# A decoder step on one core: the TensorE order of its attention fixed by the program, with other PSUM shares and another pace of the work beside it

## The chip, the cores and the metric

The kernel runs on one core of one Trainium2 chip. The metric is the device time of one execution in microseconds (us), as the median of several runs. One further execution was recorded instruction by instruction; it is called the profiled execution.

## The reference, cut to what matters

One inference step of a decoder with two layers, for two groups of tokens: a new sequence of 2048 tokens (the prompt), and 8 running sequences with 8 new tokens each (the sample), whose 4096 older positions lie in a paged cache. The first layer is recurrent. The second is attention with a forget term, for 16 heads of 64 columns; the prompt attends to itself, the sample to its cache and itself.

```python
def fox_block(q, k, v, cq, ck, q_pos, k_pos):
    s = jnp.einsum('bqhd,bkhd->bhqk', q, k).astype(jnp.float32) * (HEAD_DIM ** -0.5)
    s = s + jnp.swapaxes(cq, 1, 2)[:, :, :, None] - jnp.swapaxes(ck, 1, 2)[:, :, None, :]
    mask = k_pos[None, :] <= q_pos[:, None]
    s = jnp.where(mask[None, None], s, -jnp.inf)
    p = jax.nn.softmax(s, axis=-1)
    return jnp.einsum('bhqk,bkhd->bqhd', p.astype(v.dtype), v)
...
    return (o * jax.nn.silu(g)) @ w_out
```

All data are float32.

## The kernel before, in words

The program runs in stages: the recurrent layer, the projections to keys, values, queries and gates (with the sample's attention started beside the last of them), the prompt's attention, and the output projection. This case is about the prompt's attention, `attention` (from L1304), and the sample's, `decode` (from L1013), which runs beside it.

**The prompt's attention.** The loop at L1523 runs over 64 units (16 heads, 4 blocks of 512 query columns each), and within a unit over the key blocks k of 128 rows that the causal mask leaves: 640 steps in all, one step being one block of scores.
- *Scores* `st` (L1531, L1532, and L1534 for the mask on the diagonal): two matmuls of up to 512 columns into one PSUM bank. ScalarE takes the exponential into a tile `p` or `acc` (L1540).
- *Maxima* `sx` (`top`, L1404): before a unit's scores can be made, each of its query rows needs a maximum. One matmul of up to 512 columns into a PSUM bank is reduced by VectorE (L1406, or with the mask L1408). There are 640 of these too. `tops` gathers a unit's maxima (L1417), transposes them on TensorE (`mps`, L1421) and ScalarE writes them as rows of the queries `qbt` (L1423). `advance` issues the maxima some steps ahead of the unit that needs them, two for each step while there are any to do.
- *Products* `ops` (L1551): four steps' exponentials times the values, sixteen recorded matmuls. They are issued two steps after the fourth exponential. GpSimd adds the exponentials up (L104, `acc`), and the sums are turned into a divisor by `total` and `norm` (`tot` L1454, `rp` L1478).

**The sample's attention.** `decode` does 16 turns, 14 of them here. A turn reads 8 groups of four cache pages of keys and 8 of values, 1 MB each, into one of four buffers `raw` (DMA at L1072). VectorE transposes the keys into `ktr` (L1157); the score matmuls `dS` (L1125) and, for the new tokens, L1140 follow, then a softmax, a trip of the weights through DRAM (`pd`, `sx`), and the products `dO` (L1235), collected by `dres` (L1263). `Side.along` steps this generator forward in proportion to the cost that the loop at L1523 yields; `share` at L1796 is the proportion.

**What sets the order.** The program is written in one order, but it is built with a scheduler that runs the whole program in its own simulated time and puts on each engine, as the next instruction, one that it holds to be ready there; program order is only the priority. The result is a fixed queue for each engine. `together` (L106) keeps the matmuls of one group behind the group's first; nothing else holds TensorE's instructions in the program's order. On the chip each engine takes its queue from the front, and the DMAs are in SyncE's queue.

**PSUM.** Eight banks. The pool of the attention has six: one for `ops`, two for the scores `st`, three under the name `sx` for the maxima, `mps`, `tot` and `rp` in turn. The sample has the other two, `d` and `o`.

Of the kernel before, what the change touches and what calls it, by code (L numbers as in the profile page):

```python
# [11 lines left out]
F32 = mybir.dt.float32  # L12
# [8 lines left out]
P = 128  # L21
# [6 lines left out]
H = 16  # L28
# [16 lines left out]

SHARE = 1.13
LEAD = 18
RAMP = 8
# [4 lines left out]
FIRST = 2  # L53
NACC = 5
NP = 5
ADD = "G"
# [17 lines left out]

SYNC = mybir.DependencyInfo(mybir.DependencyClass.Sync, mybir.DependencyReason.DATA)


# [6 lines left out]
def tile_hawk_fox(  # L84
# [18 lines left out]
    def tt(eng, out, a, b, op):  # L103
        eng.tensor_tensor(out, a, b, op=op)  # L104

    def together(mms, after=()):  # L106

        first = mms[0]().ins
        for d in after:
            tc.add_manual_dep(first, d.ins.name, SYNC)  # L110
        with tc.high_priority(), tc.issue_after(first):
            for mm in mms[1:]:
                mm()

# [96 lines left out]
    psum = {}  # L211
# [1095 lines left out]
    def attention(es):  # L1307
# [3 lines left out]
        ops2 = ps3.tile([P, 512], F32, name="ops", tag="ops", bufs=1)  # L1311
        ps3.tile([P, 512], F32, name="st", tag="st", bufs=2)
        pool.tile([P, 512], F32, name="acc", tag="acc", bufs=NACC)
# [80 lines left out]
        def top(u, j, ck):  # L1394
# [7 lines left out]
            w = 512 if ck < qc else (j + 1) * P  # L1402
            ps = ps3.tile([P, 512], F32, name="sx", tag="sx", bufs=3)
            T.matmul(ps[:, :w], qb[0:96, j * P:(j + 1) * P], kb[0:96, ck * 512:ck * 512 + w], start=True, stop=True)  # L1404
            if ck < qc:
# [7 lines left out]
        def tops(u):  # L1413

            h, qc = units[u]
            m = mrows[u % 2]
            V.tensor_reduce(m[:, :4], mxs.pop(u)[:, :, :qc + 1], axis=AX.X, op=ALU.max)  # L1417

            def row():
                ps = ps3.tile([P, 512], F32, name="mps", tag="sx", bufs=3)  # L1420
                T.transpose(ps[:, :P], m[:, :], ident[:, :])  # L1421
                for j in range(4):
                    A.mul(qbs[u % NQ][96:100, j * P:(j + 1) * P], ps[:4, :P], less[:, j:j + 1])  # L1423

            later.after(1, row)
# [23 lines left out]
        def total(h2, sums, todo, single):  # L1449


            ps = ps3.tile([P, 512], F32, name="tot", tag="sx", bufs=3)
            for qc, acc in todo:
# [11 lines left out]
        def norm(pr, sums, q0, n, oT):  # L1465
# [10 lines left out]
            def gate(qc, sg):  # L1476
                ps = ps3.tile([P, 512], F32, name="rp", tag="sx", bufs=3)
# [43 lines left out]
        ops = acc = None  # L1521
        pair = []
        for u, (h, qc) in enumerate(units):  # L1523
            load_low(u + 2)
            for k in range(nks[u]):
# [3 lines left out]
                ks = slice(k * P, (k + 1) * P)  # L1529
                ps = ps3.tile([P, 512], F32, name="st", tag="st", bufs=2)  # L1530
                T.matmul(ps[:, lo:], ka[:, ks], qa[:, lo:], start=True, stop=False)  # L1531
                T.matmul(ps[:, lo:], kb[:, ks], qb[:, lo:], start=False, stop=(k < qc * 4))  # L1532
# [42 lines left out]

    lent = {}

# [18 lines left out]
    def project(es):  # L1596
# [22 lines left out]
        def post(i, pool, yps, x1, y):  # L1619
# [9 lines left out]
            if i < len(rows) - 1:  # L1629
# [9 lines left out]
                     y=lent["out"][:, :, :].rearrange("p k d -> p (k d)"),  # L1639
                     ps=lambda j: lent["psum"].tile([P, 512], F32, name="y", tag="st", bufs=2))]  # L1640

# [153 lines left out]
    psum["att"] = banks(att, "psa", 6)  # L1795
    side.along(attention(att), share)  # L1796
    side.upto(1e12)
# [38 lines left out]
```

## Time and profile before

| | us |
|---|---|
| three runs | 3064.86, 3054.63, 3062.46 |
| their median | 3062.46 |
| the profiled execution | 3055.27 |
| its span, from the first to the last instruction | 3053.6 |
| TensorE (PE) busy in the span | 2827.0 (93%) |
| VectorE (DVE) busy | 1810.2 (59%) |
| ScalarE (ACT) busy | 1269.8 (42%) |
| GpSimd (POOL) busy | 1079.6 (35%) |
| the prompt's attention, about | 1715 to 2850 in the span |
| the sample's last product in it | 2559.9 |

In the lines of the profile, L1404 is line 1404 of the kernel before; `out<-in` are the program's names of tiles. Busy time of PE is modelled from the matmul's size, and matmuls overlap, so two of them in a row show 0.39 us each while they start 0.23 us apart. "PEclk" is the share of the full TensorE clock that was granted. A wait is an idle time of an engine and what ended it.

### The profile page before, as it was taken

What the parts mean: (1) busy time and instruction counts of PE and PEld (TensorE: products, weight loads), DVE (VectorE), ACT (ScalarE), POOL (GpSimd) and SP (SyncE); (2) the same over time, 40 slices, a digit from 0 to 9 for tenths busy, and PEclk for the clock granted to TensorE, in tenths of its full rate; (3) what the DMA queues carried; (4) which work ended last, traced back from release to release, by engine and by line L of the source; (5) the groups of instructions that cost most, each with busy time, mean ns of one, the idle gap of its engine ahead of it and who ended that gap; (6) DMA issues with size and microseconds to landing.
All of it is one profiled execution on the core that took longest, in us unless ns stands there. A gap on an engine that the chain in (4) does not pass through costs nothing.

```text
span 3053.6 us, 60463 instructions
## 1 busy us (share of the span) xinstructions
PE 2827.0 (93%) x21614; PEld 2258.5 (74%) x21614; DVE 1810.2 (59%) x4012; ACT 1269.8 (42%) x2874; POOL 1079.6 (35%) x1199
## 2 busy tenths in 40 slices
PE   6998999999999989998999799899899899999898
PEld 5997789988999978896888456565556565565687
DVE  7876465425357766765555566676767675554344
ACT  4665442222346655433333144343444345455311
POOL 1653201000016532000000366556465557587522
PEclk9999999999999999999999799899999999999999
DMA  4224546788622256999999988999999998323243
GB/s 122 81 85 133 175 125 203 240 268 263 216 83 89 83 185 194 316 320 320 330 311 315 294 274 268 299 275 308 306 298 319 322 297 258 92 65 86 84 145 111
DMA packets 492864, 653.41 MB, mean 214 GB/s; under 512 B 91099, under 2 KB 292828, under 8 KB 485285
## 3 DMA queue, kind: packets, MB, share of 16 engines
q1 hardware_dynamic: 488934, 643.87, 67.1%
q10 hardware_dynamic: 3340, 3.56, 0.5%
q8 instruction: 171, 2.80, 0.4%
q0 software_dynamic: 288, 2.10, 0.2%
q14 instruction: 131, 1.07, 0.1%
HBM read 513.82 MB, written 135.16 MB: 213 GB/s over the span
## 4 chain that ended last, share of the span: by engine, by line
PE 59%; DMA 18%; DVE 9%; ACT 5%; SPq 4%; issue 3%; POOL 2%; DVEq 0%; ACTq 0%; POOLq 0%
PE ops L1551 6%; PE y L368 4%; PE y L366 4%; PE y L367 4%; DMA raw<-in_cache_v_dram 4%; PE kv L366 4%; PE kv L367 4%; PE kv L368 4%; DMA raw<-in_cache_k_dram 4%; PE st L1531 3%; PE sx L1404 3%; PE dO L1235 3%; PE dS L1125 2%; PE st L1532 2%; PE qg L366 2%
## 5 line engine op out<-in xcount | busy, mean ns | idle before, releaser
L104 POOL TENSOR_TENSOR acc<-acc,p 128x512 f32<-128x512 f32 (+3 forms) x576 | 638.7, 1109 | 419.2 <-PE ops L1551 271.1
L1540 ACT ACTIVATE p<-st 128x512 f32<-128x512 f32 (+3 forms) x576 | 289.5, 524 | 404.9 <-PE st L1532 198.8
L1157 DVE STREAM_TRANSPOSE ktr<-raw 128x1024 f32<-128x1024 f32 x256 | 305.7, 1225 | 160.2 <-DMA raw<-in_cache_k_dram 157.8
L1406 DVE TENSOR_REDUCE mxs<-sx 128x1 f32<-128x512 f32 x384 | 253.1, 679 | 119.7 <-PE sx L1404 118.3
L367 PE MATMUL kv<-wl,xh 128*128 128x256 f32 (+3 forms) x1088 | 309.3, 287 | 11.2 <-DVE wl L411 11.0
L366 PE MATMUL kv<-wh,xh 128*128 128x256 f32 (+3 forms) x1088 | 310.8, 290 | 5.9 <-ACT wh L410 5.4
L368 PE MATMUL kv<-wh,xl 128*128 128x256 f32 (+3 forms) x1088 | 309.4, 287 | 0.0
L1531 PE MATMUL st<-qa,ka 128*128 128x512 f32 (+3 forms) x640 | 273.9, 428 | 12.2 <-ACT p L1540 11.0
L1551 PE MATMUL ops<-p,vvt 128*64 128x256 f32 (+1 forms) x2176 | 261.0, 366 | 3.4 <-ACT p L1540 2.8
L1404 PE MATMUL sx<-kbt,qbt 96*128 96x512 f32 (+3 forms) x640 | 236.9, 425 | 26.1 <-DMA qbt<-qd 12.0
L1532 PE MATMUL st<-qbt,kbt 128*128 128x512 f32 (+3 forms) x640 | 239.3, 374 | 0.0
L410 ACT ACTIVATE wh<-wst,gv 128x256 fp32r<-128x256 f32 (+1 forms) x384 | 164.5, 499 | 179.9 <-DMA wst<-in_b_w_in_dram 62.1
L411 DVE SCALAR_TENSOR_TENSOR wl<-wst,gv,wh 128x256 fp32r<-128x256 f32 (+1 forms) x384 | 170.5, 493 | 105.5 <-ACT wh L410 104.0
L1551 PEld LDWEIGHTS ops<-p,vvt 128*64 128x64 f32 x2176 | 161.2, 140 | 92.6 <-issue 22.7
L366 PE MATMUL qg<-xh,wh 128*128 128x384 f32 (+2 forms) x640 | 228.9, 359 | 0.0
L368 PE MATMUL qg<-xh,wl 128*128 128x384 f32 (+2 forms) x640 | 227.4, 356 | 0.0
L367 PE MATMUL qg<-xl,wh 128*128 128x512 f32 (+2 forms) x640 | 226.9, 356 | 0.0
L367 PEld LDWEIGHTS kv<-wl,xh 128*128 128x128 f32 (+1 forms) x1088 | 204.3, 189 | 14.9 <-DVE wl L411 12.6
L366 PEld LDWEIGHTS kv<-wh,xh 128*128 128x128 f32 (+1 forms) x1088 | 204.2, 189 | 12.0 <-ACT wh L410 6.4
L1090 POOL TENSOR_TENSOR qw<-qb,amask 128x128 f32<-128x128 f32 x64 | 29.3, 464 | 509.9 <-PE dS L1125 266.4
L368 PEld LDWEIGHTS kv<-wh,xl 128*128 128x128 f32 (+1 forms) x1088 | 205.6, 189 | 4.1 <-issue 4.1
L1531 PEld LDWEIGHTS st<-qa,ka 128*128 128x128 f32 x640 | 124.0, 194 | 109.9 <-issue 53.0
(297 smaller groups left out, 6370.0 us busy)
## 6 DMA issues: line engine op xcount, KB each, us to landing
raw<-in_cache_k_dram SPq DMA_DIRECT2D x512, 256.0 KB
raw<-in_cache_v_dram SPq DMA_DIRECT2D x512, 256.0 KB
wst<-in_w_kv_dram SPq DMA_DIRECT2D x48, 512.0 KB
wst<-in_b_w_in_dram SPq DMA_DIRECT2D x48, 512.0 KB
xt<-in_x_prompt_dram SPq DMA_DIRECT2D x32, 512.0 KB
wst<-in_a_w_in_dram SPq DMA_DIRECT2D x64, 256.0 KB
out_dram<-kf SPq DMA_DIRECT2D x128, 128.0 KB
sc<-cd SPq DMA_DIRECT2D x16, 1024.0 KB
```

The source lines that it names most:

```text
L104: eng.tensor_tensor(out, a, b, op=op)
L366: T.matmul(ps, lh(k), rh(k), start=(k == 0), stop=False)
L367: T.matmul(ps, lh(k), rl(k), start=False, stop=False)
L368: T.matmul(ps, ll(k), rh(k), start=False, stop=(k == nk - 1))
L411: V.scalar_tensor_tensor(wl[:, k, :], st[:, k, :], gk, f(wh[:, k, :]), op0=ALU.mult, op1=ALU.subtract)
L1157: V.transpose(t.kts[pp][:, n], raw[:, :, pp * 256:(pp + 1) * 256])
L1404: T.matmul(ps[:, :w], qb[0:96, j * P:(j + 1) * P], kb[0:96, ck * 512:ck * 512 + w], start=True, stop=True)
L1406: V.reduce_max(mx[:, j, ck:ck + 1], ps[:, :w], axis=AX.X)
L1531: T.matmul(ps[:, lo:], ka[:, ks], qa[:, lo:], start=True, stop=False)
L1532: T.matmul(ps[:, lo:], kb[:, ks], qb[:, lo:], start=False, stop=(k < qc * 4))
L1540: pair.append((k, lo, p, A.activation(p[:, lo:], ps[:, lo:], AF.Exp)))
L1551: return T.matmul(ops[r * HD:(r + 1) * HD, a0 * P:], vvs[h % 2][:, k, :], p[:, :].rearrange("p (a r c) -> p a r c", a=2, r=2)[:, a0:, r, : ...
```

## The change

Four things, all from the start of the prompt's attention on. Before it, the instructions of every engine stand as they did.

1. **TensorE's order.** A list `line` holds the last matmul, and `behind` puts the next one behind it, by a dependence that costs no semaphore (`NoSync`). It is called for the scores' first matmul, for every maximum, and for the first matmul of each `together` group, so for the products and for the sample's `dS` and `dO` too. Not in this line are `mps`, `tot`, `rp`, the sample's small matmuls (`dm`, `dsum`, `dres`) and the output projection.
2. **PSUM.** Three banks for the scores instead of two, two under the name `sx` instead of three. Once the sample is done, every fourth block of scores uses the sample's bank `d`.
3. **Tiles.** Six tiles `p` instead of five.
4. **Pace.** The sample's steps are spread so that what is left of them ends at 88% of the attention's cost, instead of by a fixed share.

```diff
+SPAN = 0.88
...
-NP = 5
+NP = 6
...
+ORDER = mybir.DependencyInfo(mybir.DependencyClass.NoSync, mybir.DependencyReason.DATA)
...
+    line = []
+
+    def behind(ins):
+
+        if line:
+            if line[0] is not None:
+                tc.add_manual_dep(ins, line[0].name, ORDER)
+            line[0] = ins
+
     def together(mms, after=()):
 
         first = mms[0]().ins
         for d in after:
             tc.add_manual_dep(first, d.ins.name, SYNC)
+        behind(first)
         with tc.high_priority(), tc.issue_after(first):
             for mm in mms[1:]:
-                mm()
+                last = mm().ins
+        if line:
+            line[0] = last
...
-        ps3.tile([P, 512], F32, name="st", tag="st", bufs=2)
+        ps3.tile([P, 512], F32, name="st", tag="st", bufs=3)
...
-            ps = ps3.tile([P, 512], F32, name="sx", tag="sx", bufs=3)
-            T.matmul(ps[:, :w], qb[0:96, j * P:(j + 1) * P], kb[0:96, ck * 512:ck * 512 + w], start=True, stop=True)
+            ps = ps3.tile([P, 512], F32, name="sx", tag="sx", bufs=2)
+            behind(T.matmul(ps[:, :w], qb[0:96, j * P:(j + 1) * P], kb[0:96, ck * 512:ck * 512 + w], start=True, stop=True).ins)
...
+        wide = [0]
+
+        def scores_bank():
+
+            if dec_done:
+                wide[0] += 1
+                if wide[0] % 4 == 0:
+                    return psum["dec"].tile([P, 512], F32, name="st", tag="d", bufs=1)
+            return ps3.tile([P, 512], F32, name="st", tag="st", bufs=3)
+
...
-                ps = ps3.tile([P, 512], F32, name="st", tag="st", bufs=2)
-                T.matmul(ps[:, lo:], ka[:, ks], qa[:, lo:], start=True, stop=False)
+                ps = scores_bank()
+                first = T.matmul(ps[:, lo:], ka[:, ks], qa[:, lo:], start=True, stop=False)
+                behind(first.ins)
...
         dec.close()
+        dec_done.append(True)
...
-    side.along(attention(att), share)
+    line.append(None)
+    cost = sum(4.1 * 0.42 * (512 - max(0, k - qc * 4) * P) + 213 for qc in range(4) for k in range(4 * qc + 4)) * H
+    side.along(attention(att), ((16 - FIRST) * TURN - side.spent) / (cost * SPAN))
```

The line numbers move: the scores' matmuls are L1555, L1557 and L1559 in the changed kernel, the maxima L1418, the products L1576, the sample's `dS` L1139, `dO` L1249 and L1257, `dres` L1277.

**First place: TensorE in the fourth unit of the first head.** The scores of this unit read `qbt_19540`; `sx` rows make the maxima of a later unit, `ops` are products, `dm` is a transpose of the sample's softmax. Before:

```order
L1531 MATMUL st<-qa,ka 128x512
L1532 MATMUL st<-qbt_19540,kbt_19537 128x512
L1177 MATMUL dm<-ident,dmx 128x128
L1404 MATMUL sx<-kbt_19537,qbt_19541 128x512
L1531 MATMUL st<-qa,ka 128x512
L1532 MATMUL st<-qbt_19540,kbt_19537 128x512
L1404 MATMUL sx<-kbt_19537,qbt_19541 128x512
L1531 MATMUL st<-qa,ka 128x512
L1532 MATMUL st<-qbt_19540,kbt_19537 128x512
L1531 MATMUL st<-qa,ka 128x512
L1532 MATMUL st<-qbt_19540,kbt_19537 128x512
```

The same unit in the changed kernel, where `dS` and `dO` are the sample's groups of score and product matmuls:

```order
L1555 MATMUL st<-qa,ka 128x512
L1557 MATMUL st<-qbt_19540,kbt_19537 128x512
L1418 MATMUL sx<-kbt_19545,qbt_19542 128x512 x2
L1249 MATMUL dO<-raw,sx 32x256 x8
L1555 MATMUL st<-qa,ka 128x512
L1557 MATMUL st<-qbt_19540,kbt_19537 128x512
L1418 MATMUL sx<-kbt_19545,qbt_19542 128x512
L1418 MATMUL sx<-kbt_19545,qbt_19542 128x256
L1139 MATMUL dS<-ktr,qw 32x128 x32
L1555 MATMUL st<-qa,ka 128x512
L1557 MATMUL st<-qbt_19540,kbt_19537 128x512
L1418 MATMUL sx<-kbt_19545,qbt_19542 128x512 x2
```

Before, one or no maximum stands between two blocks of scores here, where the scheduler found a place. Now two stand behind each block while a unit has any to do, as the program writes them, and the sample's groups stand where the program's side generator was stepped.

**Second place: TensorE at the end of the sample,** its last products `dO<-raw` (cached rows) and `dO<-rawn` (new rows). Before, this is among the scores of the eleventh head:

```order
L1404 MATMUL sx<-kbt_19545,qbt_19540 128x512 x2
L1235 MATMUL dO<-raw,sx 32x256 x8
L1243 MATMUL dO<-rawn,dpc_13798 32x256 x2
L1531 MATMUL st<-qa,ka 128x512
L1532 MATMUL st<-qbt_19539,kbt_19537 128x512
```

Now it is among those of the fourteenth head:

```order
L1418 MATMUL sx<-kbt_19545,qbt_19539 128x256
L1249 MATMUL dO<-raw,sx 32x256 x8
L1555 MATMUL st<-qa,ka 128x512
L1557 MATMUL st<-qbt_19543,kbt_19545 128x512
L1257 MATMUL dO<-rawn,dpc_13798 32x256 x2
```

Counted over the whole queue, 437 of the 640 blocks of scores stand ahead of the sample's last group before, and 541 now. A block's score pair directly between two pairs of maxima occurs 8 times before and 107 times now.

More of the change, by code (lines that the diff above doesn't have):

```diff
@@ L1419, in row @@
             def row():
-                ps = ps3.tile([P, 512], F32, name="mps", tag="sx", bufs=3)
+                ps = ps3.tile([P, 512], F32, name="mps", tag="sx", bufs=2)
                 T.transpose(ps[:, :P], m[:, :], ident[:, :])
@@ L1449, in total @@
         def total(h2, sums, todo, single):
-            ps = ps3.tile([P, 512], F32, name="tot", tag="sx", bufs=3)
+            ps = ps3.tile([P, 512], F32, name="tot", tag="sx", bufs=2)
             for qc, acc in todo:
@@ L1476, in gate @@
             def gate(qc, sg):
-                ps = ps3.tile([P, 512], F32, name="rp", tag="sx", bufs=3)
+                ps = ps3.tile([P, 512], F32, name="rp", tag="sx", bufs=2)
                 T.matmul(ps[:, :], sel[:, qc, :], rr[:, :], start=True, stop=True)
@@ L1574, in attention @@
                 yield 4.1 * (512 - lo) * 0.42 + (done[0] - before) * 213
-    lent = {}
+    lent, dec_done = {}, []
     rows = [(NSAMP, None, x1s_d[:, :], ys_flat)]
@@ L1639, in project @@
                      y=lent["out"][:, :, :].rearrange("p k d -> p (k d)"),
-                     ps=lambda j: lent["psum"].tile([P, 512], F32, name="y", tag="st", bufs=2))]
+                     ps=lambda j: lent["psum"].tile([P, 512], F32, name="y", tag="st", bufs=3))]
         def part(i, fn, *names):
```

## The prediction

> **What bounds the kernel now.** I read the page first, then the busy time by stretch, then who TensorE (PE) waited for, then single stretches. The page shows one engine close to full:
>
> ```profile
> span 3053.6 us, 60463 instructions
> PE 2827.0 (93%) x21614; PEld 2258.5 (74%) x21614; DVE 1810.2 (59%) x4012; ACT 1269.8 (42%) x2874; POOL 1079.6 (35%) x1199
> ```
>
> The change touches only the prompt's attention, so I cut that in two: the stretch with the sample beside it, which ends with the sample's last product, and the tail without it. The columns are busy time of PE, PE's weight loads, DVE, ACT and POOL, then PE's granted clock, the DMA engines' busy share and GB/s.
>
> ```profile
> L1235 PE MATMUL dO<-raw,sx x1376: 376/379/637, 1721.2 to 2559.9; 128*32 128x256 f32 x197
> ...
> 1715.00:2575.00 860.00, 791.05 (x7633) 501.78 (x7634) 573.51 (x1178) 361.42 (x916) 473.80 (x463) 0.95 0.95 296
> 2575.00:2850.00 275.00, 258.17 (x1458) 156.58 (x1456) 131.95 (x303) 142.45 (x318) 207.81 (x183) 0.98 0.32 86
> ```
>
> PE is the bound in both. What an order can win is its idle time and its lost clock. In the first stretch PE is idle for 860 - 791.05 = 69 us, and a clock of 0.95 is worth at most 0.05 x 860 = 43 us; in the tail it is 17 us and 0.02 x 275 = 5.5 us. So **about 135 us are in play**, and no change of order or banks alone can win more. The waits say whose they are. First the stretch with the sample, then the tail:
>
> ```profile
> PE dO L1235 <- DMA raw<-in_cache_v_dram: 18.7, 14, 3.3
> PE sx L1404 <- DVE mxs L1406: 7.2, 12, 2.3
> PE mps L1421 <- DVE mrow L1417: 7.2, 5, 3.8
> PE dO L1235 <- issue: 5.1, 3, 3.5
> PE dS L1125 <- DVE ktr L1157: 4.4, 4, 2.7
> PE dS L1140 <- DVE sc L104: 4.3, 3, 2.3
> PE st L1531 <- ACT p L1540: 3.5, 11, 0.5
> PE dO L1235 <- DMA raw<-in_cache_k_dram: 3.3, 2, 1.7
> PE sx L1404 <- ACT qbt L1423: 3.2, 8, 0.8
> PE dO L1235 <- DMA sx<-pd: 3.2, 3, 1.3
> ```
>
> ```profile
> PE st L1531 <- ACT p L1540: 7.5, 14, 1.2
> ```
>
> The reader is to see three kinds. The sample's groups (`dO`, `dS`) wait for pages and transposes: 18.7 + 5.1 + 4.4 + 4.3 + 3.3 + 3.2 = 39.0 us. The maxima and their transposes wait for DVE and ACT: 7.2 + 7.2 + 3.2 = 17.6 us. The scores wait for a bank that ACT reads: 3.5 + 7.5 = 11.0 us.
>
> **The change part by part.**
>
> *The sample's groups pinned, and their pace.* The sample's last group moves from behind block 437 of 640 to behind block 541, so the same transfers spread over 541/437 = 1.24 times as many steps. The DMA engines are busy 0.95 x 860 = 817 us of the first stretch. The tail shows what the prompt's attention asks for alone, a share of 0.32, or 275 us of those 860; so the sample has 542 us. With 99 blocks left for the tail at 275/203 = 1.35 us each, the stretch with the sample becomes some 960 us, and its DMA share 542/960 + 0.32 = 0.88. That leaves slack where there was hardly any, but the groups now stand where the program writes them, and a late page holds everything behind it. I take half of the 39.0 us as saved, **-19.5** (estimate; ends -39.0 and 0).
>
> *The clock.* It follows long gaps. Here is one, on PE's timeline, and the 10 us stretches around it:
>
> ```profile
> 1940.80 0.50 PE L1404 MATMUL sx<-kbt,qbt 96*128 96x512 f32 x1 [0.70 <-DVE mxs L1406]
> 1945.10 0.48 PE L1421 MATMUL mps<-ident,mrow 128*128 128x128 f32 x1 [3.80 <-DVE mrow L1417]
> ```
>
> ```profile
> 1930.00:1940.00 10.00, 9.18 (x57) 5.46 (x53) 8.30 (x18) 4.07 (x14) 4.96 (x7) 1.00 0.70 214
> 1940.00:1950.00 10.00, 4.54 (x12) 2.83 (x11) 8.73 (x24) 4.44 (x16) 0.00 (x0) 0.59 1.01 268
> 1950.00:1960.00 10.00, 9.82 (x42) 6.20 (x44) 4.49 (x9) 2.11 (x4) 0.00 (x0) 0.50 0.98 322
> ```
>
> A 3.8 us wait costs a second time: for the next ten and more microseconds PE looks full and does half the work. The scheduler had put maxima and a transpose in a row there, and no scores between them. The Trainium skill, page "TensorE: Matmul & The Clock Gate", section "Why this matters for your kernels", says to allow no idle gap over about 3 us between bursts of matmuls, or the clock halves; this trace agrees (3.8 us, then 0.50). A pinned order puts two maxima behind a block of scores and never a dozen in a row, but for the first unit. The start of the attention stays as it is, with its clock:
>
> ```profile
> 1715.00:1725.00 10.00, 5.33 (x24) 2.49 (x24) 2.87 (x9) 2.10 (x8) 0.00 (x0) 0.50 1.03 355
> 1725.00:1735.00 10.00, 9.67 (x48) 6.65 (x52) 6.87 (x14) 4.35 (x10) 2.19 (x3) 0.74 0.98 340
> ```
>
> That is 0.5 x 5.33 + 0.26 x 9.67 = 5 us of the 43, so 38 us can go. I take two thirds, **-25** (estimate; ends -38 and 0, since a late page can still make such a gap).
>
> *Three banks for the scores, six tiles p.* The 11.0 us of waits for ACT go, since a third bank gives ACT one more block's time: **-11** (ends -11 and 0). The borrowed bank `d` adds a fourth in the tail, for nothing more. The sixth tile `p` helps ACT, which waited for POOL's additions; ACT is busy 361 of 860 us, so that wait is covered, and I put it at 0. If it weren't, it would have shown among the scores' waits, counted above:
>
> ```profile
> ACT p L1540 <- POOL acc L104: 19.3, 16, 2.8
> ```
>
> *Maxima in pairs, on two banks.* This is the part that costs. PE's own pace first, from starts on its timeline, and the durations of DVE's work by line in the first stretch:
>
> ```profile
> 2321.85 0.39 PE L1532 MATMUL st<-qbt,kbt 128*128 128x512 f32 x1
> 2322.08 0.39 PE L1531 MATMUL st<-qa,ka 128*128 128x512 f32 x1
> 2322.31 0.39 PE L1532 MATMUL st<-qbt,kbt 128*128 128x512 f32 x1
> 2322.54 0.39 PE L1404 MATMUL sx<-kbt,qbt 96*128 96x512 f32 x1
> 2322.86 1.07 PE L1235 MATMUL dO<-raw,sx 128*32 128x256 f32 x16
> ```
>
> ```profile
> L1406 DVE TENSOR_REDUCE mxs<-sx 128x1 f32<-128x512 f32 x280 | 184.0, 676 | 65.9 <-PE sx L1404 65.2
> L1157 DVE STREAM_TRANSPOSE ktr<-raw 128x1024 f32<-128x1024 f32 x148 | 177.2, 1226 | 78.2 <-DMA raw<-in_cache_k_dram 75.8 <-DMA raw<-in_cache_v_dram 1.9 <-DMA r<-rs 0.2
> L1408 DVE CUSTOM_DVE_ANT_0 sx<-sx,maskb 128x512 f32<-128x512 f32 (+3 forms) x177 | 85.5, 491 | 53.2 <-PE sx L1404 52.8
> L1408 DVE DVE_READ_ACCUMULATOR2_ANT mxs<- 128x1 f32 x177 | 24.3, 137 | 0.0
> ```
>
> A matmul of 512 columns starts 0.23 us after its like and some 0.32 us after one of another shape. Two maxima and a block of scores are four of them, 0.92 to 1.10 us; the two reductions take DVE 2 x 0.676 = 1.35 us. With two banks, the next pair can't start before the last pair is reduced, so PE stalls 0.25 to 0.43 us at each of the 107 places where one block of scores stands alone between two pairs: 27 us by the lower. DVE also does other things, nearly all the sample's: 573.5 - 184.0 - 85.5 - 24.3 = 279.7 us, which over 960 us is 0.29 of its time. In 107 x 1.35 = 144 us of such places it claims 42 us, of which I take half as hidden: sixteen product matmuls come after every fourth step, and DVE has them to itself:
>
> ```profile
> 1831.73 1.88 PE ops L1551 x16
> ```
>
> So 27 + 21 = 48 us, and 5 us more where `mps`, `tot` or `rp` hold one of the two banks: **+53** in place of the 17.6 us that the maxima cost now, **-17.6**. Below, the scheduler arranges DVE's queue to the pinned order as well as it does now, and the cost stays 17.6. Above, each of the 107 places stalls 0.43 us and half of a 1.226 us transposition: 107 x 1.04 = 111, with the 5 us 116.
>
> *Fewer changes of shape.* The maxima stand in 386 groups before and 321 after, counted in the two queues. 65 changes fewer, at 0.32 - 0.23 = 0.09 us: **-6** (ends -12, if the way back costs it too, and 0).
>
> *What only moves.* `mps`, `tot`, `rp` and the output projection stay free. 89 matmul rows of the projection filled the tail before, 24 do now; 65 x 0.23 = 15 us of work go from ahead of the last scores to behind them and change no sum. DVE, ACT and POOL get other orders, but PE is the bound, and they count only where PE waits for them.
>
> The sum: -19.5 - 25 - 11 - 17.6 - 6 + 53 = -26 us. The profiled execution took 3055.27 us (span 3053.6 and 1.7 around it), which makes **3029 us**. The median of the runs shown is 7 us above that execution, so against 3062.46 a median of 3029 would be a little more than these terms give.
>
> **The rivals.**
>
> *A. Two banks make DVE the bound: slower.* For it: the 107 places, where DVE has 1.35 us of work for 0.92 to 1.10 us of PE's, and DVE's own wait for the sample's keys, 75.8 us in the row of L1157, which with two banks reaches PE sooner. Against it: DVE is busy only 574 of 860 us, and the products give it pauses. At the upper end (116) and with long gaps left, so that no clock is won: -19.5 - 11 - 17.6 - 6 + 116 = +62, 3117 us; with the clock won, +37, 3092 us. It decides from 79 us of stalls, or (79 - 5)/107 = 0.69 us at each place. The Trainium skill, page "Perfetto Trace Analysis", section "Optimization Strategy", holds a gap that keeps repeating on the engine that should be full for a sign of too little PSUM; here that would be this rival, and no run before shows it.
>
> *B. The sample's late pages hold the whole queue: slower.* The scheduler may place a sample's group later; the pinned order can't. If its 39.0 us double and no clock is won: +39 - 17.6 - 11 - 6 + 53 = +57, 3113 us. For it: `dO` stands half a turn of the generator behind its fetch. Against it: four buffers `raw`, and a DMA share of 0.88.
>
> *C. Nothing to measure.* Runs of this kernel can tell about 0.3% (9 us) from no change. The stalls at DVE eat what the gaps gave, 79 us in all: 3055 us.
>
> *D. Far more.* The scheduler, told PE's order, fits DVE's queue to it, and every other term comes out at its end: -39 - 38 - 11 - 12 = -100, 2955 us.
>
> **How the numbers follow.** The forecast, 3000 to 3046 us, 0.38; D 0.14; C 0.13; A 0.24; B 0.11. Faster by over 0.3% is the forecast and D, 0.52; the same is C, 0.13; slower is A and B, 0.35. The range reaches into D and into A and B until about 0.2 is left out: 2965 to 3105.
>
> **What would show it.** Right: PE's waits for `raw` about 20 us in all; no idle gap of 3 us after 1740; the clock at 0.98 or more with the sample; waits of PE `sx` for DVE `mxs` many, short, 30 to 60 us in sum; waits of `st` for ACT near nothing; the sample's last `dO` some 960 us after 1715; the last scores near 2825. Wrong: `sx` waiting for DVE over 80 us (A); `dO` or `dS` as the largest wait of PE (B); a part of the queue before 1715 that takes another time than it did.

## The result and the profile after

| | before | changed |
|---|---|---|
| median of the runs (4 each), us | 3062.45 | 3300.84 (3294.82 to 3319.08) |
| ratio, 95% interval | | 1.0793 [1.0746, 1.084] |
| span of the profiled execution, us | 3053.6 | 3297.1 |
| the last block of scores ends, us | 2867 | 3100 |
| PE idle from 1715 to there, us | 86 | 225 |
| PE busy from 1715 to there, us | 1066 | 1161 |
| from there to the end of the span, us | 187 | 197 |

The change costs 238 us (median); the prediction said 3029 us, 33 us less than before. The first two rows of its page, of engines and of the clock's 40 slices (the sample runs beside the attention from slice 21 to 36):

```profile
span 3297.1 us, 60495 instructions
PE 2925.3 (89%) x21614; PEld 2290.8 (69%) x21614; DVE 1815.2 (55%) x4012; ACT 1269.0 (38%) x2874; POOL 1074.9 (33%) x1199
...
PEclk9999999999999999989987988898989889989999
```

The same matmuls are recorded, 21614, yet PE is busy 98 us longer: a lower clock stretches them. The busy time by stretch, columns as in the prediction, cut at the sample's last product and at the last scores, for before and then for the changed kernel:

```profile
1715.00:2561.00 846.00, 777.05 (x7543) 492.31 (x7544) 563.75 (x1157) 352.64 (x898) 464.57 (x454) 0.95 0.95 297
2561.00:2867.00 306.00, 288.69 (x1629) 177.52 (x1628) 148.31 (x332) 156.78 (x349) 225.49 (x198) 0.98 0.34 94
```

```profile
1715.00:2937.00 1222.00, 1019.04 (x8353) 615.68 (x8355) 648.03 (x1337) 426.88 (x1068) 572.64 (x552) 0.88 0.72 218
2937.00:3100.00 163.00, 141.47 (x779) 85.51 (x776) 70.17 (x149) 78.71 (x171) 108.85 (x95) 0.95 0.29 84
```

These four rows account for the loss. PE's idle time goes from 69 + 17 = 86 us to 203 + 22 = 225, so **+138**. The clock's loss, one minus the granted share times the stretch, as the prediction counted it, goes from 0.05 x 846 + 0.02 x 306 = 48 us to 0.12 x 1222 + 0.05 x 163 = 155, so **+107**; some 15 us of the output projection left the stretch, which makes +92 of the 95 us more busy time. (This loss counts half clock while PE stood idle, too. Over the time in which PE was busy alone, the clock records give 42 us before and 131 us after, +90.) And the end grows by 10 us, where that projection went. 138 + 95 + 10 = 243, the growth of the span. The DMA share fell from 0.95 to 0.72.

Who PE waits for in the changed kernel, from 1715 to the last scores (us in total, times, longest):

```profile
PE sx L1418 <- DVE mxs L1420: 99.5, 91, 8.7
PE sx L1418 <- DVE mxs L1422: 38.0, 29, 6.2
PE ops L1576 <- ACT p L1565: 19.8, 29, 2.6
PE rp L1492 <- DMA r<-rs: 17.7, 4, 10.8
PE sx L1418 <- DMA qbt<-qd: 13.7, 1, 13.7
PE sx L1418 <- DVE sgt L106: 6.9, 12, 1.4
PE mps L1435 <- DVE mrow L1431: 5.0, 5, 1.7
```

The maxima wait 99.5 + 38.0 = 137.5 us for VectorE's reductions; before, the like rows held 8.6 us. The waits are few and long, 120 of 1.15 us in the mean. Some 94 us of them stand at a maximum that has only a block of scores between itself and the last pair, the place that the prediction priced. Behind these rows, `rp` waits 17.7 us for a transfer of the divisors, 0.6 before, for which the prediction had no term. The 13.7 us row ends at 1715 and is not in the 225. Here is one of 4.37 us, PE's timeline and then DVE's:

```profile
2088.18 0.65 PE L1418 MATMUL sx<-kbt,qbt 96*128 96x384 f32 x2
...
2093.51 0.80 PE L1418 MATMUL sx<-kbt,qbt 96*128 96x512 f32 x1 [4.37 <-DVE mxs L1422]
```

```profile
2087.82 0.69 DVE L106 TENSOR_TENSOR sc<-dS,sc 128x512 f32<-128x512 f32 x1 [1.09 <-PE dS L1139]
2088.43 1.24 DVE L1171 STREAM_TRANSPOSE ktr<-raw 128x1024 f32<-128x1024 f32 x1
2090.58 2.37 DVE L1171 STREAM_TRANSPOSE ktr<-raw 128x1024 f32<-128x1024 f32 x2 [0.91 <-DMA raw<-in_cache_k_dram]
2092.87 0.53 DVE L1422 CUSTOM_DVE_ANT_0 sx<-sx,maskb 128x384 f32<-128x384 f32 x1
```

PE filled both banks by 2088.8. VectorE reaches the first reduction at 2092.87: four instructions of the sample stand ahead of it, one of which waits 0.91 us for a page of keys. PE's queue holds the next maximum in front of everything else, so it stands still. Adding up what VectorE does during all of PE's 170.7 us of idle time before `sx` (each of its instructions cut to the gap): reductions 75 us, the sample's key transposes 54, waiting for the sample's pages 20, the sample's other steps 13, work for the prompt and the output projection 10 (the rest is smaller; records overlap a little). This says what stood there, not what each of them costs.

### The profile page after: what moved, and what is told of

It is laid out like the page before. It is cut to its first block, busy times and chain, and to the rows that moved or that the text cites. A ratio compares the mean times of both kernels' runs of the same rounds, so it can differ in the third digit from the quotient of the medians.

```text
span 3297.1 us, 60495 instructions
## 1 busy us (share of the span) xinstructions
PE 2925.3 (89%) x21614; PEld 2290.8 (69%) x21614; DVE 1815.2 (55%) x4012; ACT 1269.0 (38%) x2874; POOL 1074.9 (33%) x1199
## 5 line engine op out<-in xcount | busy, mean ns | idle before, releaser
L1418 PE MATMUL sx<-kbt,qbt 96*128 96x512 f32 (+3 forms) x640 | 270.7, 470 | 170.7 <-DVE mxs L1420 99.5
L1418 PEld LDWEIGHTS sx<-kbt,qbt 96*128 96x128 f32 x640 | 131.7, 214 | 278.8 <-DVE mxs L1420 155.8
L1576 PE MATMUL ops<-p,vvt 128*64 128x256 f32 (+1 forms) x2176 | 287.3, 393 | 9.2 <-ACT p L1565 8.6
L1555 PE MATMUL st<-qa,ka 128*128 128x512 f32 (+3 forms) x640 | 282.9, 443 | 7.4 <-DMA qa<-qd 4.1
L1576 PEld LDWEIGHTS ops<-p,vvt 128*64 128x64 f32 x2176 | 175.0, 151 | 110.6 <-issue 32.2
L1557 PE MATMUL st<-qbt,kbt 128*128 128x512 f32 (+3 forms) x640 | 247.9, 387 | 0.0
L1555 PEld LDWEIGHTS st<-qa,ka 128*128 128x128 f32 x640 | 131.5, 205 | 106.8 <-issue 81.3
```

The costliest lines, as they stand in the source:

```text
L1418: behind(T.matmul(ps[:, :w], qb[0:96, j * P:(j + 1) * P], kb[0:96, ck * 512:ck * 512 + w], start=True, stop=True).ins)
L1555: first = T.matmul(ps[:, lo:], ka[:, ks], qa[:, lo:], start=True, stop=False)
L1576: return T.matmul(ops[r * HD:(r + 1) * HD, a0 * P:], vvs[h % 2][:, k, :], p[:, :].rearrange("p (a r c) -> p a r c", a=2, r=2)[:, a0:, r, : ...
```

## The experiments

All runs at a glance. "Idle" is PE's from 1715 to the last scores, "half clock" the part of it behind 1740 in which the trace's clock records stand at a half; both are from the profiled execution. Each ratio is to runs of the kernel before on the same chip.

| what differs | us | ratio [95%] | idle | half clock |
|---|---|---|---|---|
| before | 3062 | | 87 | 82 |
| changed kernel | 3301 | 1.0793 [1.0746, 1.084] | 238 | 290 |
| e1, three banks for maxima | 3221 | 1.0522 [1.0471, 1.0572] | 191 | 215 |
| e2, no order | 3172 | 1.0359 [1.0329, 1.0389] | 153 | 236 |
| e3, maxima not in the order | 3202 | 1.0458 [1.0397, 1.0518] | 171 | 263 |
| e4, sample not in the order | 3215 | 1.05 [1.0428, 1.0573] | 188 | 203 |
| e5, before + order alone | 3305 | 1.0791 [1.0719, 1.0862] | 182 | 176 |
| e6, before + banks alone | 3184 | 1.0396 [1.0346, 1.0446] | 164 | 253 |
| e7, before + pace alone | 3068 | 1.0027 [1.0009, 1.0045] | 99 | 68 |
| e8, one maximum a step | 3259 | 1.0639 [1.0608, 1.067] | 222 | 288 |
| e9, keys wait for no page | 3310 | 1.0821 [1.0794, 1.0847] | 241 | 283 |
| e10, short reductions | 3213 | 1.0503 [1.0477, 1.053] | 193 | 212 |
| e12, order of scores and products only, old banks for maxima | 3049 | 0.9961 [0.9945, 0.9976] | 91 | 75 |
| e13, before + tiles and borrowed bank | 3058 | 0.9992 [0.9976, 1.0007] | 99 | 75 |
| e14, e12 + maxima in the order | 3161 | 1.0323 [1.0293, 1.0353] | 161 | 163 |
| e15, e12 + sample in the order | 3083 | 1.0093 [1.0023, 1.0163] | 102 | 113 |
| e16, e12 with two banks for maxima | 3194 | 1.0433 [1.0403, 1.0463] | 172 | 229 |
| e17, no key transposes | 3195 | 1.0447 [1.0421, 1.0473] | 167 | 174 |
| e18, reductions first | 3311 | 1.0826 [1.08, 1.0853] | 241 | 294 |

The idle column adds gaps one by one, the one that began ahead of 1715 with its whole length, and comes out up to 14 us above the windows' difference. The expectations number their theories in the order in which these came up.

### One part undone (e1 to e4, from the changed kernel)

e1 gives the maxima back their third bank and takes it from the scores:

```diff
-name="st", tag="st", bufs=3
+name="st", tag="st", bufs=2
...
-name="sx", tag="sx", bufs=2
+name="sx", tag="sx", bufs=3
```

> The changed kernel with the PSUM shares as before (three banks for the maxima, two for the scores); the pinned order, the tiles and the pace stay. Theory 1 (the pinned maxima wait for their two banks, because VectorE's queue is held up): a third bank gives most of the 137 us of waits of sx for VectorE back and the clock with them, about 3120 us, and sx <- DVE mxs below 60 us. Theory 2 (it is the sample's groups in the pinned order, which give the page buffers back late and so make the pages late): near 3290 us, the scores waiting for ACT a little more.

3221.48 us, between the two theories. The third bank takes the maxima's waits for VectorE from 137.5 to 92.6 us, far from the 8.6 of before, so the step from three banks to two makes about a third of it.

e2 takes the order away and keeps banks, tiles and pace:

```diff
-    line.append(None)
```

> The changed kernel without the pinned order (the list stays empty); banks, tiles and pace stay as changed. Theories 1 and 2 both put the loss on the pinned order: about 3060 to 3080 us. Theory 3 (two banks for the maxima or the wider pace cost the time whatever the order): 3200 us or more, with sx <- DVE mxs still over 80 us.

3171.56 us, again between the two. More than half of the loss goes with the order, and 109 us stay. What waits there is another thing: `dO` for pages, 48.5 us, with 32.2 us of `sx` for VectorE.

e3 leaves the maxima out of the order, e4 the sample's groups:

```diff
-            behind(T.matmul(ps[:, :w], ...).ins)
+            T.matmul(ps[:, :w], ...)
```

> The changed kernel with the maxima taken out of the pinned order; scores, products and the sample's groups stay in it. Theory 1: the scheduler puts the maxima where VectorE is free, about 3080 us, sx <- DVE mxs below 40 us. Theory 2: 3250 us or more, since the sample's groups are still pinned.

```diff
-    def together(mms, after=()):
+    def together(mms, after=(), held=True):
...
-        behind(first)
+        if held:
+            behind(first)
...
-        if line:
+        if line and held:
             line[0] = last
...
-                together([partial(score, h, x, a) ...])
+                together([partial(score, h, x, a) ...], held=False)
...
```

> The changed kernel with the sample's groups (dS, dO) taken out of the pinned order; scores, maxima and products stay in it. Theory 1: near 3280 us, the waits of sx for VectorE as they are. Theory 2: about 3120 us, with SyncE's waits for PE dO (114 us in the changed kernel) and VectorE's for key pages (129 us) down to what they were before.

3201.82 and 3214.89 us, and again neither theory's numbers. Each alone gives back 99 and 86 us, and each still has 81 and 61 us of `sx` waiting for VectorE. The four gains of e1 to e4 (79, 129, 99, 86) add up to more than the loss: the parts hurt together.

### One part alone (e5 to e7, from the kernel before)

e5 adds `line` and `behind` only (banks 2 and 3, five tiles, the old share); e6 only the banks, `st` 3 and `sx` 2; e7 only the last line:

```diff
-    side.along(attention(att), share)
+    cost = sum(...) * H
+    side.along(attention(att), ((16 - FIRST) * TURN - side.spent) / (cost * SPAN))
```

> The kernel before with the pinned order alone: three banks for the maxima, two for the scores, five tiles p, the old share for the sample, no borrowed bank. If the parts of the change cost about what they cost in the runs so far (the order 129 us on top of the rest, the rest 109 us without it), 3130 to 3190 us, with waits of sx for VectorE of 60 to 100 us. If the order only hurts together with two banks: within 20 us of 3062.

> The kernel before with the PSUM shares alone: two banks for the maxima, three for the scores; the scheduler's order, five tiles p and the old share. If the 109 us of the run without the pinned order are the second bank's: 3150 to 3180 us. If they are the pace's: near 3062.

> The kernel before with the sample's pace alone (88% of the attention's cost); scheduler's order, old banks, five tiles p. If the pace is harmless, because the scheduler runs the sample ahead anyway (in the run without the pinned order its last product came at 2589 us, against 2560 before): 3050 to 3080 us. If it is the pace that costs: 3150 us or more.

3305.35, 3184.41 and 3068.13 us. The order alone costs as much as the whole change, more than was expected, and in part for a reason of its own. The last scores come 75 us later than before, with 82.4 us of `sx` waiting for VectorE; and at the old share the held sample trails behind the attention. Its stretches, to the last scores and from there to its last product:

```profile
1715.00:2942.00 1227.00, 1045.04 (x8094) 643.74 (x8094) 644.94 (x1385) 493.10 (x1191) 675.78 (x642) 0.92 0.64 191
2942.00:3088.00 146.00, 68.58 (x1006) 44.77 (x1008) 54.07 (x93) 10.31 (x41) 3.47 (x8) 0.67 0.88 292
```

For these 146 us PE is half idle at a clock of 0.67; the largest wait there is `dO` for pages, 48.1 us. So the new pace belongs to the order: without the order it gains nothing (1.0027), and e1, which differs from e5 by pace, tiles and borrowed bank, is 84 us better.

The banks alone cost 124 us in the scheduler's own order. Its stretches:

```profile
1715.00:2603.00 888.00, 759.92 (x7125) 481.07 (x7124) 529.55 (x1066) 310.72 (x806) 405.31 (x400) 0.88 0.89 279
2603.00:2995.00 392.00, 356.46 (x2011) 222.17 (x2010) 184.44 (x429) 191.61 (x434) 279.76 (x248) 0.93 0.31 82
```

The sample takes about as long as before (888 for 846 us), but 381 blocks of scores start beside it in the trace, not 436: the fixed queue that the scheduler makes for two banks has fewer of them there. The other 55, at 306/204 = 1.5 us each, are 83 us of tail. Beside the sample PE waits more, too: `dO` for pages 48.3 us, not 18.7, and the clock is at 0.88. e6 moves one bank from the maxima to the scores, as every run with two banks here does; whether the bank taken or the bank given costs the time was not tried.

### Why the maxima wait so long (e8, e9, e10, e17, e18, from the changed kernel)

e8 issues the maxima one a step instead of two, to be done up to 9 steps ahead of their unit instead of 18. Hardly a pair is left, 2 for 300:

```diff
-start[u] + nks[u] - 2 * max(0, start[u] - min(LEAD, RAMP + tick) - tick)
+start[u] + nks[u] - max(0, start[u] - min(9, RAMP + tick) - tick)
```

> The changed kernel with the maxima issued one for each step instead of two, and up to 9 steps ahead of their unit instead of 18; all else as changed, two banks, pinned order. If it is the pairs that VectorE can't follow (1.35 us of reductions for 0.92 us of matmuls): sx <- DVE from 137 us to below 60, and 3200 us or less. If it is VectorE's queue being held by late key pages, whatever the spacing: 3260 us or more, single waits of several us as before.

3259.03 us, 42 us less; the waits fall from 137.5 to 96.1 us. That lies between the two theories: pairs are part of it and not the main part.

e9 asks whether the late pages of keys, for which VectorE waits 129 us, hold the reductions behind them. The key transposes beside the attention read a constant there, and the sample's result is left out:

```diff
-                    V.transpose(t.kts[pp][:, n], raw[:, :, pp * 256:(pp + 1) * 256])
+                    if ahead:
+                        V.transpose(t.kts[pp][:, n].rearrange("p a (b c) -> p (a b) c", c=P),
+                                    ident[:, :].unsqueeze(1).to_broadcast([P, 8, P]))
+                    else:
+                        V.transpose(t.kts[pp][:, n], raw[:, :, pp * 256:(pp + 1) * 256])
```

> The changed kernel in which the sample's key transposes read a constant tile instead of the page that came (the pages are still fetched; the sample's result is left out). VectorE does the same work and never waits for a key page (129 us of waits in the changed kernel). Theory 4 (a late key page holds VectorE's queue, the reductions behind it hold the two banks, and the pinned TensorE stands): sx <- DVE from 137 us to below 70, single waits below 3 us, 3190 us or less. Rival (VectorE's work alone, in pairs, is too much): sx <- DVE stays over 110 us, 3260 us or more.

3310.43 us. VectorE never waits for a page of keys there, and PE's maxima still wait 119.3 us for it. So the loss doesn't need the late pages, and theory 4 fell. What they cost in the changed kernel isn't shown: the scheduler made another queue for VectorE in e9, with about a quarter of its instructions elsewhere.

e10 cuts the reductions to the last 64 columns (128 on the diagonal) and, as these maxima may be too small, adds 20 to them (one more step of 0.33 us for each unit):

```diff
-                V.reduce_max(mx[:, j, ck:ck + 1], ps[:, :w], axis=AX.X)
+                V.reduce_max(mx[:, j, ck:ck + 1], ps[:, 448:], axis=AX.X)
...
```

> The changed kernel with maxima taken over the last 64 columns of a block (128 on the diagonal) plus 20 instead of over all columns; the rest of each block is left out of the maximum. VectorE's work on maxima falls from 416 us to some 150; its waits for pages stay. Rival (VectorE's work is too much): sx <- DVE below 60 us, 3200 us or less. Theory 4: sx <- DVE still 90 us or more with single waits over 5 us, 3240 us or more.

3213.42 us. One reduction takes 0.218 us for 0.682, VectorE is busy 480.57 us for 648.03 in the stretch, and the waits are 73.0 us, again between the theories.

e17 leaves the key transposes out altogether: one transposed tile, made once, serves all turns beside the attention, and the sample's result is left out again.

```diff
-                    t.kts = [pool.tile([P, 4, 4, 256], F32, name="ktr", tag="ktr", bufs=nktr) for _ in range(2)]
+                    if not (ahead and kept):
+                        t.kts = [pool.tile([P, 4, 4, 256], F32, name="ktr", tag="ktr", bufs=nktr) for _ in range(2)]
+                        if ahead:
+                            kept.append(t.kts)
...
+                    else:
+                        t.kts = kept[0]
...
+                    if not ahead:
...
```

> The changed kernel, with the key transposes beside the attention left out: one tile made once from a constant serves all of the sample's score matmuls, so VectorE does 1.2 us less for each of them and never waits for a page of keys (the sample's result is left out by that; every matmul and every transfer stays). In the run in which the key transposes read a constant, VectorE waited for no page, TensorE's maxima still waited 119 us for VectorE and the time was 3310 us; in 71 us of the maxima's waits VectorE was at work on those transposes. Theory 5, that the maxima wait because the sample's transposes stand ahead of the reductions in VectorE's queue: the maxima's waits for VectorE fall by some 70 us to 50, and with their echo in the clock the time falls by 70 to 150 us, to 3160 to 3240 us. Rival, that two banks and a 0.68 us reduction for each 0.23 us matmul are enough by themselves: the waits stay at 100 or more, and the time above 3270 us.

3195.03 us, 115 less than e9. The stretch with the sample, and the waits in it:

```profile
1715.00:2829.00 1114.00, 967.97 (x8353) 588.38 (x8353) 483.56 (x1183) 427.30 (x1069) 572.47 (x552) 0.92 0.78 238
```

```profile
PE sx L1430 <- DVE mxs L1432: 45.9, 74, 3.9
PE rp L1504 <- DMA r<-rs: 42.9, 6, 11.4
PE ops L1588 <- ACT p L1577: 17.0, 25, 2.4
PE sx L1430 <- DVE sgt L106: 10.9, 14, 2.9
PE sx L1430 <- DVE mxs L1434: 8.4, 24, 1.6
```

The maxima wait 45.9 + 8.4 = 54.3 us, as theory 5 said. Beside e10 this shows that both kinds of work on VectorE make them wait: 167 us less of its time in the stretch is worth 88 us as reductions, and 161 us less 115 us as transposes, though VectorE was busy for only 648 of 1222 us. The reading that fits is that what counts is how much work stands between two maxima in its queue; no run varied that place alone.

e18 marks the reductions as first wherever the scheduler holds them to be ready:

```diff
-            if ck < qc:
...
+            with tc.high_priority():
+                if ck < qc:
...
```

> The changed kernel, with its reductions marked as first in VectorE's queue wherever the scheduler holds one to be ready. Theory 5: fewer of the sample's transposes stand ahead of a waiting reduction; the maxima's waits for VectorE fall below 110 us and the time by 20 to 100 us, unless the scheduler's simulated time holds the reductions to be late where on the chip they are not, in which case nothing moves by more than 20 us. Rival, that the reductions' own duration sets the waits: no change beyond 20 us.

3310.72 us; the waits are 136.1. The two traces say why nothing moves: VectorE's instructions stand in the same order in e18 as in the changed kernel, from the start of the attention to the end. The mark changed no place in the queue, which fits the reservation in theory 5, and so e18 says nothing for or against its rival.

### Which part of the order (e12 to e16)

e12 is the changed kernel with only scores and products in the order, and two banks for `st`, three for `sx`; that is e1, e3 and e4 together. e13 is the kernel before with six tiles and the borrowed bank. e14 and e15 put the maxima, or the sample's groups, back into e12's order by the edits of e3 and e4 reversed; e16 is e12 with e1's edit reversed.

> Only scores and products in the pinned order; maxima and the sample's groups free; PSUM shares as before; six tiles p, the borrowed bank and the new pace. Theory: pinning what needs VectorE or pages is what costs, so 3050 to 3090 us, half clock below 110 us. Rival (any pinned order costs, since it takes the scheduler's freedom to fill): 3130 us or more.

> The kernel before with six tiles p and, once the sample is done, every fourth block of scores in the sample's bank d; nothing else of the change. The scores' waits for ACT were 7.5 us in the tail: 3050 to 3062 us.

> Three banks for the maxima; scores, products and maxima in the pinned order, the sample's groups free; tiles, borrowed bank and pace as changed. With neither pinned 3049 us was measured, with both 3221. If the maxima carry the loss: 3180 us or more, sx <- DVE over 60 us. If the sample's groups carry it: below 3100 us. If the two only hurt together: below 3080.

> The same with the sample's groups in the pinned order and the maxima free. If the sample's groups carry the loss: 3180 us or more, with SyncE waiting for PE dO over 60 us and VectorE for key pages over 100 us. If the maxima carry it: below 3100 us. If the two only hurt together: below 3080.

> Scores and products pinned, maxima and sample free, as in the run that took 3049 us, but with two banks for the maxima and three for the scores. If the second bank costs by itself what it cost in the scheduler's order (122 us alone): 3150 us or more, with waits of sx for VectorE and of dO for pages up. If it only cost beside an order made for three: below 3090.

Medians in us, all with the scores and products in the order, the new pace, six tiles and the borrowed bank:

| in the order, too | three banks for maxima | two banks |
|---|---|---|
| nothing | 3049 (e12) | 3194 (e16) |
| sample | 3083 (e15) | 3202 (e3) |
| maxima | 3161 (e14) | 3215 (e4) |
| both | 3221 (e1) | 3301 (changed) |

On three banks the sample in the order costs 34 us (its runs spread from 3076 to 3102), the maxima 112, both 172. Two banks instead of three cost 145 us with nothing else held and less with more held (119, 54, 80), each time with the bank given to the scores. e12 against e16, by stretch:

```profile
1715.00:2573.00 858.00, 781.23 (x7549) 494.19 (x7550) 559.38 (x1164) 351.44 (x898) 465.83 (x455) 0.95 0.94 295
2573.00:2848.00 275.00, 261.41 (x1560) 165.66 (x1559) 134.87 (x313) 152.20 (x342) 216.14 (x192) 0.99 0.35 94
```

```profile
1715.00:2593.00 878.00, 748.59 (x7119) 470.83 (x7111) 530.67 (x1063) 304.46 (x805) 406.02 (x400) 0.89 0.89 280
2593.00:2995.00 402.00, 359.56 (x1987) 224.42 (x1985) 181.07 (x414) 186.86 (x433) 275.50 (x248) 0.92 0.28 76
```

With the same pace and the same held instructions, 381 blocks instead of 436 start beside the sample, and 127 of the 145 us are the longer tail: 55 blocks more, and each slower (402/259 = 1.55 us for 275/204 = 1.35). So part of a bank's price lies in the queue that the scheduler makes, before the chip runs it. The same 145 us can be added up by engine: PE is idle 172 us instead of 91 and at half clock 229 instead of 75, and its maxima wait 48.6 us for VectorE instead of 8.1. No run separates the queue from these waits.

e14 shows the same shape without a bank less. It missed its forecast: the maxima in the order cost 112 us, but `sx` waits for VectorE only 27.7 us in it, where over 60 was expected. Its stretches:

```profile
1715.00:2562.00 847.00, 719.25 (x6990) 455.41 (x6989) 525.84 (x1060) 302.90 (x777) 388.90 (x385) 0.90 0.91 286
2562.00:2961.00 399.00, 365.80 (x2122) 225.07 (x2118) 176.43 (x420) 207.42 (x463) 295.86 (x262) 0.99 0.34 92
```

The sample ends no later than in e12, and the tail is 124 us longer: 361 blocks start beside the sample, not 436. (In e4, with two banks, it is 315.) So with the sample free the loss shows as blocks that no longer stand beside it. When the sample's groups are held as well, the waits of the maxima for VectorE grow, from 27.7 to 92.6 us on three banks (e14, e1) and from 61.4 to 137.5 on two (e4, changed).

e12 is the fastest of all: 3049.08 us, ratio 0.9961 [0.9945, 0.9976], a gain of 0.4%. What it owes to the order of the scores and what to the pace, which alone gives 1.0027, wasn't taken apart; six tiles and the borrowed bank are worth nothing that shows (e13).

## Why the prediction was wrong

**What bounds it: right, and misread.** PE was the bound, and 135 us the most that an order could win. The prediction took this as the field of play, and priced losses only by waits it could already see. It has no such limit downwards: idle time and lost clock came to 138 + 107 = 245 us more.

**The sample's groups, -19.5: their waits fell, and the price lay elsewhere.** The prediction's rows of `dO` and `dS` add up to 39.0 us; now `dO` waits 1.1 for pages of values and 1.6 otherwise, and `dS` at L1139 2.7 for `cn`. But e15 shows +34 us for holding the groups on three banks, and e4 86 us on two with the maxima held, where the maxima's waits are 137.5 us with the groups held and 61.4 without. That holding them puts the sample's VectorE work in front of the reductions fits the example above and was not tried by itself. The slack forecast for the DMA engines came (0.72, forecast 0.88), but in a stretch of 1222 us, not 960, and the pages' queue itself waited for `dO` to free buffers:

```profile
SPq L1086 <- PE dO L1249: 114.1, 26, 12.0
```

**The clock, -25: the wrong sign, and the step that failed second.** It came to +107. The step said that the clock follows long gaps and that a pinned order has none, and both halves failed. Behind 1740 the changed kernel has 14 gaps of 3 us or more (up to 10.8 us; the kernel before has 2). And most half clock needs none: 30 of the changed kernel's 44 stretches at half clock, 171 of 290 us, begin where no gap of 3 us or more touches the 7 us ahead of them. The kernel before could have said so, with 11 of its 13. Its one example was misread: PE's wait of 3.8 us runs from 1941.3 to 1945.1, and the clock is at a half from 1941.8 on. The prediction's own row of 0.59 for 1940 to 1950 says the same, for a clock that halved at 1945 would have shown 0.75. Cut there:

```profile
1930.00:1941.80 11.80, 9.78 (x58) 5.65 (x54) 10.10 (x22) 5.87 (x22) 4.96 (x7) 1.00 0.74 212
1941.80:1945.10 3.30, 0.00 (x1) 0.01 (x2) 3.30 (x12) 0.18 (x2) 0.00 (x0) 0.50 1.20 286
```

In the changed kernel, here is a place where the clock halves after two gaps of about a microsecond, PE's timeline first, then stretches of 7 us:

```profile
1907.35 0.47 PE L1418 MATMUL sx<-kbt,qbt 96*128 96x512 f32 x1
1908.61 0.50 PE L1418 MATMUL sx<-kbt,qbt 96*128 96x512 f32 x1 [0.78 <-DVE mxs L1420]
1910.12 0.50 PE L1555 MATMUL st<-qa,ka 128*128 128x512 f32 x1 [1.01 <-ACT p L1565]
```

```profile
1904.00:1911.00 7.00, 5.20 (x35) 3.33 (x34) 6.00 (x19) 6.57 (x24) 3.48 (x5) 1.00 0.80 215
1911.00:1918.00 7.00, 6.81 (x35) 4.12 (x38) 3.01 (x8) 3.06 (x10) 3.40 (x4) 0.51 0.99 316
1918.00:1925.00 7.00, 6.08 (x48) 3.33 (x40) 3.45 (x8) 1.84 (x4) 0.53 (x1) 1.00 1.00 312
```

The prediction had cited a rule on gaps over 3 us. The same page of the Trainium skill, "TensorE: Matmul & The Clock Gate", has another, in its section "A second HAM failure mode: psum-queue depth-cycling": cycling through PSUM banks idles TensorE in many small gaps, and the clock swings between half and full. This trace agrees with that one: 0.78 and 1.01 us, then 0.51. In the table of runs half clock rises with PE's idle time, from 68 to 82 us at 87 to 99 us idle to 283 to 294 us at 238 to 241, but loosely: at 161 to 172 us idle it lies anywhere from 163 to 263. That the waits cause the lost clock was not tried by itself.

**Three banks for the scores, -11: the wait moved.** `st` for ACT fell from 11.0 to 3.2 us. But the products, now at a fixed place, wait 19.8 us for the exponentials, 4.4 before. The sum is +7.6.

**Maxima in pairs, on two banks, +53: the step that failed first.** Its mechanism was right and its size wrong. The waits for the reductions alone are 137.5 us, and with the others on these banks in the rows above (6.9 and 5.0) 149, above the upper end of 116. Some 94 us of the 137.5 stand at places of the kind that it counted, 0.9 us for each of the 107, where 0.25 to 0.43 was put. What was mis-sized is VectorE's answer. The sample's work there was spread as a mean share, 0.29, and half of it counted as hidden, 21 us; it comes in bursts, four instructions ahead of a reduction in the example, and stands in 54 + 20 + 13 = 87 us of PE's gaps. Without the key transposes and their pages the waits fall to 54.3 us (e17), still twice the 27 us that were put for the pairs themselves. The second bank was priced by stalls alone; with neither maxima nor sample held the runs with two banks have 55 blocks fewer beside the sample as well (e6, e16), which could not show in a queue with the sample held.

**Fewer changes of shape, -6:** not seen by itself, and its price was read at another place, from a maximum to the sample's products. In the trace before, with PE at full clock and not idle, a maximum starts 0.23 us behind a block of scores and a block 0.24 us behind a maximum (medians of 121 and 125), but a second maximum 0.31 us behind the first. **What only moves:** the end grew by 10 us, where 15 were counted.

**The pace.** The stretch was to be 960 us with 1.35 us for each block left; it is 1222, and 163/101 = 1.6. The last scores were to end near 2825 and end at 3100.

**The rivals.** A happened, by its own sign (`sx` for DVE over 80 us) and beyond its point of decision (79 us), but at 3117 us it still held the clock to be no worse than before. With 107 us for the clock it would have been 3224. B didn't happen: `dO` hardly waits in the changed kernel, and in e5 its waits for pages, 48.1 us, lie behind the last scores. The Trainium skill's sign of too little PSUM, page "Perfetto Trace Analysis", section "Optimization Strategy", was cited under A; e16 against e12 agrees (145 us, with 48.6 us of waits of the maxima for VectorE instead of 8.1), as far as the third bank for the scores does no harm.

## What to carry to other kernels

Before an engine's order is fixed, list for each instruction that it will hold which other engine must answer, and what stands ahead of that answer in the other engine's fixed queue: a mean busy share of a half says nothing about bursts of four. Hold only the instructions whose partners are early; here that was the scores and products, not the maxima nor the sample. A wait on TensorE can cost twice, as idle time and as clock (138 and 107 us here). And look at what the scheduler's new queue puts beside the part that waits for transfers: here 381 or 361 blocks instead of 436, with no long wait to see.

## What the runs showed of the hardware that was not expected

The granted clock halves after gaps of about 1 us in a row, not only after long ones, for stretches in units of 3.4 us (3.4, 6.8, 10.2 and more in the clock records). Before, 13 such stretches made 82 us between 1740 and the last scores; in the changed kernel 44 made 290 us, 30 of them without a gap of 3 us near. A long gap, too, can begin at full clock and end at half: before, the clock fell 0.5 us into one of 3.8 us. Why a given pair of gaps trips it and another doesn't is open.
